# Convolution module of a two-layer encoder trunk: eleven more second-row taps on VectorE, and a written order for the totals, the diagonal products and the tiles at the module's end

## Chip, cores and metric

The kernel runs on one core of a Trainium2 chip. The metric is the device time in microseconds (us) of one execution, as the median of several runs.

## The reference

The program computes a trunk of two layers on 256 tokens of 1024 channels. Each layer is a feed-forward block, a mixer and a second feed-forward block, each behind an RMS norm. The mixer of the first layer is a convolution module, and the change lies in its second half:

```python
def conv_module(h, w_pw1, w_dw, g_norm, w_pw2):
    u = h @ w_pw1
    a, b = jnp.split(u, 2, axis=-1)
    u = a * jax.nn.sigmoid(b)
    u = lax.conv_general_dilated(u, w_dw[:, None, :], window_strides=(1,),
        padding=[(CONV_WIDTH - 1, 0)], feature_group_count=D_MODEL, ...)
    u = jax.nn.silu(rmsnorm(u, g_norm))
    return u @ w_pw2
```

The convolution is depthwise: each channel is the sum of 31 shifted copies of itself, each times a weight of its own. The norm needs, for each token, the sum of squares over all 1024 channels, so it can only be finished when the last channel of a token is.

## The kernel before

**Tiles.** In the module's middle the data lie with channels on partitions: eight groups k = 0 to 7 of 128 channels, and along the free axis 30 zeros and 256 tokens (tile `V`). The tokens are worked in two halves of 128, here the *first rows* (tb 0) and the *second rows* (tb 1). `Y` holds the convolution's result in the same layout.

**Who computes the taps.** A tap is one of the 31 shifted products. Three tables (lines 49 to 51 of the kernel before) give each engine its groups and taps.
- VectorE (DVE, `taps_dve`, L764 to L776): one multiply-add per tap (L775), into two accumulators `acc` in PSUM by turns, which L776 adds at the end. It has groups 0, 2, 4, 5 and taps 0 to 12 of group 7.
- ScalarE and GpSimd (ACT and POOL, `taps_pool`, L778 to L795): ACT writes each product into one of six buffers `prod` (L793), POOL adds it to `Y` or `part` and to `odd` by turns (L794), and L795 adds the two. They have groups 1, 3 and taps 0 to 18 of group 6.
- TensorE (PE, `taps_pe`, L797 to L807): a product with a diagonal matrix of the tap's weights, `diag`, summed in PSUM tile `y` (L804). It has the rest of groups 6 and 7: 12 + 18 products for each half of the tokens.

**The norm.** For a group and a half, L890 adds PE's part to the other engine's, ACT squares the result (L816, `sq`), and PE multiplies the squares with a column of ones (L822, tile `ms`): this is a *total*, and eight of them make the sum of squares of 128 tokens. Then `normed` (L835 to L854): DVE forms the mean (L838, `msc`), POOL raises it to the power -1/2 (L840, `rc`), DVE writes this on a diagonal (L842, `dg`), PE multiplies the diagonal with ones so that every partition has it (L844, `rb`), DVE multiplies each group with it (L849, `z`, six buffers), and ACT applies the Silu (L851, `Z`; for groups 0 to 3 also the rounded `Zh`, L853, whose remainder `Zl` DVE takes, L854). The groups come in the order 4 to 7, 0 to 3.

**The last product.** `mm` (L905) multiplies `Z` with the last weights, tile by tile in that order and two column halves each (L915, tile `o`); groups 0 to 3 take three passes (`lo` with `Zh`, `hi` with `Zh`, `hi` with `Zl`: L277, L280, L281). `add` (L921) adds the result to the residual `h`. The next feed-forward block then takes `h` in transposed pieces `tp` (L320, `Xh`, `Xl`), and its first two weight blocks must be split by ACT into `hi` (L164) and by DVE into `lo` (L168). `load_ahead()` calls for these.

**What sets the order.** Each engine works its own queue strictly as written in the program. A list scheduler writes these queues when the program is built, from the dependences and its own estimates. `@urgent` gives a function's instructions priority; `order(a, b)` puts a behind b on an engine, with no wait added; `behind(a)` puts a behind the last urgent instructions of its engine. Ahead of the change only few places are tied in this way: the last totals, `rb`, and two positions in the last product (L901 to L912).

Of the kernel before, what the change touches and what calls it, by code (L numbers as in the profile page):

```python
# [11 lines left out]
F32 = mybir.dt.float32  # L12
# [68 lines left out]
def trunk(ctx: ExitStack, tc: tile.TileContext, x, xt, pos, invf, gains, gfin, wdw,  # L81
# [633 lines left out]
    def conv_in(act, X, make_next):  # L715
# [37 lines left out]

        behind(nc.scalar.activation(small.tile([P, 1], F32, tag="silu", name="silu2"), neghalf, AF.Silu))
        load_to(conv_block[-4] + 1)
# [7 lines left out]

        def taps_dve(k, j0, j1, t):  # L764

            slot[0] ^= 1
            c = slice(slot[0] * S, slot[0] * S + t.stop - t.start)
            out = Y[:, k, t]
            for j in range(j0, j1):
                v, w = V[:, k, j + t.start:j + t.stop], dw[:, k, j:j + 1]  # L770
                y = acc[(j - j0) % 2][:, c]
                if j - j0 < 2:
                    nc.vector.tensor_scalar(y, v, w, None, op0=ALU.mult)
                else:
                    nc.vector.scalar_tensor_tensor(out if j == j1 - 1 else y, v, w, y, op0=ALU.mult, op1=ALU.add)  # L775
            nc.vector.tensor_add(out, acc[(j1 - j0) % 2][:, c], out)  # L776

        def taps_pool(k, j0, j1, t):  # L778

            if j1 - j0 < TAPS and k not in part:  # L780
                part[k] = act.tile([P, S], F32, name=uid("part"))
            if k not in odd:
                odd[k] = act.tile([P, S], F32, tag="odd", name=uid("odd"))
            y = [(part[k] if k in part else Y[:, k, :])[:, t], odd[k][:, t]]
            for j in range(j0, j1):
                v, w = V[:, k, j + t.start:j + t.stop], dw[:, k, j:j + 1]
                o = y[(j - j0) % 2]
                if j - j0 < 2:
                    nc.scalar.activation(o, v, AF.Copy, scale=w)
                else:  # L790
                    p = act.tile([P, S], F32, tag="prod", name=uid("prod"), bufs=6)
                    p = p[:, :t.stop - t.start]
                    nc.scalar.activation(p, v, AF.Copy, scale=w)  # L793
                    nc.gpsimd.tensor_tensor(o, o, p, op=ALU.add)  # L794
            nc.gpsimd.tensor_tensor(y[0], y[0], y[1], op=ALU.add)  # L795

        def taps_pe(t, done):  # L797

            b = bank("A", "y")
            y = {}  # L800
            for i, (k, j0, j1) in enumerate(CONV_PE):
                y[k] = b[:, i * P:(i + 1) * P]
                for j in range(j0, j1):
                    mm = nc.tensor.matmul(y[k], diag[k][:, j - j0, :], V[:, k, j + t.start:j + t.stop],  # L804
                                          start=(j == j0), stop=(j == j1 - 1))
                    done.append(mm)
            return y  # L807
# [5 lines left out]
        def square(k, t):  # L813
            if k not in sq:
                sq[k] = act.tile([P, S], F32, tag="sq", name=uid("sq"), bufs=4)
            nc.scalar.activation(sq[k][:, t], Y[:, k, t], AF.Square)  # L816

# [17 lines left out]
        def normed(tb, after=()):  # L835

            ms = small.tile([P, 1], F32, tag="msc", name=uid("msc"))
            nc.vector.tensor_scalar(ms, msb[tb][:, :1], 1.0 / D, EPS, op0=ALU.mult, op1=ALU.add)  # L838
            rc = small.tile([P, 1], F32, tag="rc", name=uid("rc"))
            nc.gpsimd.tensor_tensor(rc, ms, neghalf, op=ALU.pow)  # L840
            dg = act.tile([P, P], F32, tag="dg", name=uid("dg"), bufs=2)
            nc.vector.tensor_scalar(dg, ident, rc, None, op0=ALU.mult)  # L842
            rb = bank("AC"[tb], "rb")
# [3 lines left out]
            for k in rows_order:  # L847
                z = act.tile([P, P], F32, tag="z", name=uid("z"), bufs=6)
                nc.vector.tensor_mul(z, Y[:, k, tbs(tb)], rb[:, :P])  # L849
                g = G[:, g0 + k:g0 + k + 1]  # L850
                nc.scalar.activation(Z[:, k, tbs(tb)], z, AF.Silu, scale=g)  # L851
# [4 lines left out]
        for items, taps in ((CONV_DVE, taps_dve), (CONV_POOL, taps_pool)):  # L856
            for item in items:
                if item[0] in CONV_FIRST:
                    for tb in range(NT):
                        taps(*item, tbs(tb))  # L860
                elif item[0] not in CONV_LAST:
                    taps(*item, every)
        for k in CONV_ORDER:
# [4 lines left out]
        sums = {}  # L868
        for tb in range(NT):
            t = tbs(tb)  # L870
            for item in CONV_DVE:
                if item[0] in CONV_LAST:
                    taps_dve(*item, t)
            for item in CONV_POOL:
                if item[0] in CONV_LAST:
                    taps_pool(*item, t)
            if tb == 0:
                for k in CONV_ORDER:
                    if k not in CONV_LAST:
                        for i in range(NT):  # L880
                            total(k, i)
            y[tb] = taps_pe(t, done[tb])
        def ends(tb, after, after_row):
# [4 lines left out]
            def add():  # L888
                for k in CONV_LAST:
                    nc.vector.tensor_add(Y[:, k, t], y[tb][k], part[k][:, t] if k in part else Y[:, k, t])  # L890
                    square(k, t)
# [3 lines left out]

            add()
            normed(tb, (after_row,))


        n = len(done[1])  # L900
# [20 lines left out]
        def add(tb, d):  # L921
            c = slice(d * 512, d * 512 + 512)
            nc.vector.tensor_add(h[tb][:, c], o[tb, d], h[tb][:, c])

        nxt = None
        load_ahead()
# [260 lines left out]
    dw = const.tile([P, KT, TAPS], F32, name="dw")  # L1187
    diag = {}
    apart = ExitStack()
    dpool = apart.enter_context(tc.tile_pool(name="diag", bufs=1))  # L1190

    def diagonals():
        fetch(dw, wdw)
        for k, j0, j1 in CONV_PE:
            diag[k] = dpool.tile([P, j1 - j0, P], F32, name=f"diag{k}")
# [113 lines left out]
```

## Time and profile before

| what | us |
|---|---|
| median of 3 runs | 929.18 |
| the three runs | 929.18, 927.61, 929.3 |
| the profiled execution | 928.0 |
| its span, from the first to the last instruction | 926.2 |
| PE busy in the span | 913.4 |
| from the first totals to the next feed-forward block (243.79 to 288.43 of the span) | 44.64 |

The profile gives times from the span's start. In a timeline, a row is a run of alike instructions of one engine: its start, the time to the end of the last, line, operation, tiles, count, and in brackets how long the engine sat idle before it and what released it. A product in full float32 stands in the trace as two records, so x20 are ten products. Consecutive instructions overlap, so that the distance of two starts is less than the duration of one.

### The profile page before, as it was taken

What the parts mean: (1) busy time and instruction counts of PE and PEld (TensorE: products, weight loads), DVE (VectorE), ACT (ScalarE), POOL (GpSimd) and SP (SyncE); (2) the same over time, 40 slices, a digit from 0 to 9 for tenths busy, and PEclk for the clock granted to TensorE, in tenths of its full rate; (3) what the DMA queues carried; (4) which work ended last, traced back from release to release, by engine and by line L of the source; (5) the groups of instructions that cost most, each with busy time, mean ns of one, the idle gap of its engine ahead of it and who ended that gap; (6) DMA issues with size and microseconds to landing.
All of it is one profiled execution on the core that took longest, in us unless ns stands there. A gap on an engine that the chain in (4) does not pass through costs nothing.

```text
span 926.2 us, 12414 instructions
## 1 busy us (share of the span) xinstructions
PE 913.4 (99%) x4337; PEld 761.0 (82%) x4337; DVE 680.1 (73%) x1041; ACT 537.6 (58%) x930; POOL 222.0 (24%) x329
## 2 busy tenths in 40 slices
PE   8999999999999999999999999999999999999997
PEld 6888888898967888888888888888898778888886
DVE  5777787589975667777976667978666476667875
ACT  6965455568865554555574445655667374544643
POOL 0101232479920110232210003223200010003123
PEclk9999999999999999999999999999999999999999
DMA  9986656554324866566756765666451457774751
GB/s 338 346 280 228 222 162 227 227 183 142 133 91 154 298 230 229 183 196 210 296 218 237 231 242 174 204 215 240 182 183 46 182 206 239 252 247 144 230 181 46
DMA packets 60399, 191.58 MB, mean 207 GB/s; under 512 B 11184, under 2 KB 33328, under 8 KB 40752
## 3 DMA queue, kind: packets, MB, share of 16 engines
q1 hardware_dynamic: 59760, 190.09, 59.0%
q8 instruction: 34, 0.56, 0.2%
q10 hardware_dynamic: 576, 0.69, 0.2%
q14 instruction: 29, 0.24, 0.1%
HBM read 178.17 MB, written 12.58 MB: 206 GB/s over the span
## 4 chain that ended last, share of the span: by engine, by line
PE 89%; ACT 3%; DVE 3%; issue 1%; DMA 1%; POOL 1%; POOLq 0%; SPq 0%; ACTq 0%
PE u L281 17%; PE u L277 17%; PE u L280 17%; PE o L277 6%; PE o L280 6%; PE o L281 6%; PE gate L731 3%; PE u L731 3%; DVE lo L168 2%; PE p L277 2%; PE p L280 2%; PE p L281 2%; PE o L915 2%; ACT hi L164 1%; DMA raw<-in_f1w 1%
## 5 line engine op out<-in xcount | busy, mean ns | idle before, releaser
L168 DVE TENSOR_TENSOR lo<-raw,hi 128x1024 fp32r<-128x1024 f32 (+1 forms) x246 | 297.8, 1247 | 74.4 <-ACT hi L164 74.1
L164 ACT CAST hi<-raw 128x1024 fp32r<-128x1024 f32 (+1 forms) x250 | 248.0, 1046 | 151.7 <-PE u L281 112.3
L281 PE MATMUL u<-hi,Xl 128*128 128x512 f32 x688 | 267.8, 390 | 0.7 <-DVE Xl L338 0.7
L277 PE MATMUL u<-lo,Xh 128*128 128x512 f32 x688 | 268.1, 390 | 0.0
L280 PE MATMUL u<-hi,Xh 128*128 128x512 f32 x688 | 267.7, 389 | 0.0
L281 PEld LDWEIGHTS u<-hi,Xl 128*128 128x128 f32 x688 | 129.1, 188 | 28.3 <-DVE Xl L338 1.6
L277 PEld LDWEIGHTS u<-lo,Xh 128*128 128x128 f32 x688 | 129.1, 188 | 27.2 <-DVE lo L168 0.5
L280 PEld LDWEIGHTS u<-hi,Xh 128*128 128x128 f32 x688 | 129.1, 188 | 26.6
L178 POOL TENSOR_TENSOR sums<-raw 128x1024 f32<-128x1024 f32 x20 | 53.0, 2652 | 161.2 <-DMA raw<-in_f2w 54.7
L277 PE MATMUL o<-lo,Gh 128*128 128x512 f32 (+1 forms) x236 | 91.0, 386 | 0.0
L281 PE MATMUL o<-hi,Gl 128*128 128x512 f32 (+1 forms) x236 | 91.0, 386 | 0.0
L280 PE MATMUL o<-hi,Gh 128*128 128x512 f32 (+1 forms) x236 | 91.0, 385 | 0.0
L625 POOL TENSOR_TENSOR sx<-gb 128x128 f32<-128x128 f32 x20 | 10.2, 508 | 311.6 <-DMA gb<-gd 311.6
L617 ACT CAST Gh<-gb 128x512 fp32r<-128x512 f32 (+2 forms) x48 | 25.6, 540 | 54.6 <-DMA gb<-gd 54.6
L187 DVE TENSOR_TENSOR lo<-sums,hi 128x1024 fp32r<-128x1024 f32 x40 | 56.1, 1433 | 0.0
L618 DVE TENSOR_TENSOR Gl<-gb,Gh 128x512 fp32r<-128x512 f32 (+2 forms) x48 | 33.2, 705 | 28.8 <-ACT Gh L617 28.8
L775 DVE SCALAR_TENSOR_TENSOR acc<-V,dw,acc 128x256 f32<-128x256 f32 (+1 forms) x160 | 53.9, 418 | 0.0
L186 ACT CAST hi<-sums 128x1024 fp32r<-128x1024 f32 x40 | 40.7, 1051 | 22.6 <-PE u L281 15.0
L281 PEld LDWEIGHTS o<-hi,Gl 128*128 128x128 f32 x236 | 44.3, 188 | 9.0
L277 PEld LDWEIGHTS o<-lo,Gh 128*128 128x128 f32 x236 | 44.3, 188 | 8.9
L280 PEld LDWEIGHTS o<-hi,Gh 128*128 128x128 f32 x236 | 44.3, 188 | 8.8
L186 ACT CAST hi<-raw 128x512 fp32r<-128x512 f32 (+1 forms) x40 | 31.4, 834 | 32.9 <-PE o L281 26.6
(247 smaller groups left out, 1347.4 us busy)
## 6 DMA issues: line engine op xcount, KB each, us to landing
raw<-in_f2w SPq DMA_DIRECT2D x66, 1024.0 KB, 4.9
raw<-in_f1w SPq DMA_DIRECT2D x64, 1024.0 KB, 5.0
raw<-in_cw SPq DMA_DIRECT2D x12, 1024.0 KB, 5.1
gd<-gt SPq DMA_DIRECT2D x160, 64.0 KB, 2.6
gb<-gd SPq DMA_DIRECT2D x40, 256.0 KB, 2.9
raw<-in_wo SPq DMA_DIRECT2D x4, 1024.0 KB, 4.8
raw<-in_wuq SPq DMA_DIRECT2D x3, 1024.0 KB, 4.8
raw<-in_f1w SPq DMA_DIRECT2D x8, 256.0 KB, 6.7
```

What stands on the lines that cost most here:

```text
L164: behind(nc.scalar.copy(hi[:, c], raw[:, c]))
L168: behind(nc.vector.tensor_sub(lo[:, c], raw[:, c], hi[:, c].bitcast(F32)))
L178: behind(nc.gpsimd.tensor_tensor(t[:, 0:2, :], v[:, 0:4:3, :], v[:, 1:2, :].to_broadcast([P, 2, 512]), op=ALU.add))
L186: behind(nc.scalar.copy(hi[:, c0:c1], x[:, c0:c1]))
L187: behind(nc.vector.tensor_sub(lo[:, c0:c1], x[:, c0:c1], hi[:, c0:c1].bitcast(F32)))
L277: mm = nc.tensor.matmul(o, ah, bl, start=start, stop=False)
L280: nc.tensor.matmul(o, ah, bh, start=False, stop=False)
L281: return nc.tensor.matmul(o, al, bh, start=False, stop=stop)
L617: nc.scalar.copy(dh, x)
L618: nc.vector.tensor_sub(dl, x, dh.bitcast(F32))
L731: mm = nc.tensor.matmul(u[:, t], w[:, c], X.x[:, k, t], start=(k == 0), stop=(k == KT - 1))
L775: nc.vector.scalar_tensor_tensor(out if j == j1 - 1 else y, v, w, y, op0=ALU.mult, op1=ALU.add)
```

## The change

- **Taps.** The tables get a fourth column: the half of the tokens (0, 1, or 2 for both). In the second rows, group 7 gives taps 13 to 23 from PE to VectorE: PE has 12 + 7 products there in place of 12 + 18, VectorE 24 taps in place of 13.
- **Diagonal.** `dg` is written by ScalarE (Copy with a scale) and no longer by VectorE.
- **PE's order.** The diagonal products of the first rows come right behind the module's first half, with the totals of groups 3 and 5 at fixed places among them (`CONV_MID`); the second rows' products follow, and behind the fifth of them come the last totals of the first rows, behind the fourteenth `rb`.
- **VectorE's order.** The second-row taps of group 7 are tied one behind the other. The first comes behind the first rows' `Y`, the fifth behind the mean, the tenth behind the last `z` of the first rows.
- **ScalarE and GpSimd.** Products and their sums keep one order through all groups. From the second rows' tap 10 on, products come behind `dg` and sums behind the power. `odd` has a buffer each for even and odd groups. The load of the Silu table comes behind the seventh-tap product of group 6.
- **Second rows' norm.** It is called at the seventh of eight groups of the last product (before: at the third), so that the last totals, `rb` and the tiles of the second rows come later; `load_ahead()` and the first rows' `add` come behind them.

The core of the diff, without the lines that only pass a return value on:

```diff
-CONV_DVE = ((0, 0, 31), (2, 0, 31), (4, 0, 31), (5, 0, 31), (7, 0, 13))
-CONV_POOL = ((1, 0, 31), (3, 0, 31), (6, 0, 19))
-CONV_PE = ((6, 19, 31), (7, 13, 31))
+CONV_DVE = ((0, 0, 31, 0), (0, 0, 31, 1), (2, 0, 31, 2), (4, 0, 31, 2), (5, 0, 31, 2), (7, 0, 13, 0), (7, 0, 24, 1))
+CONV_POOL = ((1, 0, 31, 0), (1, 0, 31, 1), (3, 0, 31, 2), (6, 0, 19, 0), (6, 0, 19, 1))
+CONV_PE = ((6, 19, 31, 0), (7, 13, 31, 0), (6, 19, 31, 1), (7, 24, 31, 1))
+CONV_MID = {3: 10, 5: 29}
...
+                if j in after:
+                    order(ins, after[j].ins)
+                if j > j0 and after:
+                    order(ins, before.ins)
...
-                odd[k] = act.tile([P, S], F32, tag="odd", name=uid("odd"))
+                odd[k] = act.tile([P, S], F32, tag=f"odd{k % 2}", name=uid("odd"))
...
+                    if last_prod[0] is not None:
+                        order(prod, last_prod[0].ins)
+                        order(ins, last_sum[0].ins)
+                    if "power" in after and j >= j0 + 10:
+                        order(prod, after["diagonal"].ins)
+                        order(ins, after["power"].ins)
...
-            nc.vector.tensor_scalar(dg, ident, rc, None, op0=ALU.mult)
+            diagonal = nc.scalar.activation(dg, ident, AF.Copy, scale=rc)
...
+        taps(0)
+        order(silu, nc_silu[0].ins)
+        for k in CONV_ORDER:
+            if k not in CONV_LAST:
+                if k == [*CONV_MID][0]:
+                    y[0] = taps_pe(0, done[0])
+                    order(done[0][0], mm.ins)
+                for i in range(NT):
+                    mm = total(k, i)
+                    if k in CONV_MID:
+                        order(mm, done[0][CONV_MID[k]].ins)
...
-        ends(0, done[1][n // 2 + 1], done[1][n * 3 // 4 + 1])
+            steps_of.update({0: a, 4: mean, 9: z, "power": power, "diagonal": diagonal})
...
+        ends(0, done[1][4], done[1][13])
+        order(done[1][5], sums[0].ins)
+        order(done[1][14], brow[0].ins)
+        taps(1)
...
-                after = {4: [sums[1]], 6: [brow[1]]}[n] if n in (4, 6) else ()
+                after = [brow[1]] if n == KT - 1 else ()
...
-                if tb == 0 and f == 0:
+                if tb == 0 and f == 4:
                     first = now
-                if tb == 0 and f == 2:
-                    ends(1, first[1], now[1])
+                if tb == 0 and f == KT - 2:
+                    last_z = ends(1, first[1], now[1])
+                    load_ahead()
```

What this does to the queues is seen at three places. On PE, at the end of the first rows' norm, stood before (y_2542 are the second rows' products, ms_2429 the first rows' totals):

```order
L804 MATMUL y_2542<-V,diag_445 128x128 x10
L804 MATMUL y_2542<-V,diag_695 128x128 x5
L822 MATMUL ms_2429<-ones,sq_2574 128x1
L804 MATMUL y_2542<-V,diag_695 128x128 x3
L822 MATMUL ms_2429<-ones,sq_2577 128x1
L804 MATMUL y_2542<-V,diag_695 128x128 x10
L844 MATMUL rb_2587<-dg_2585,ones 128x128
L915 MATMUL o_2637<-raw_1908,Z 128x512
```

Now the same place on PE reads as follows (y_2474 are the second rows' products, and two more of them stand ahead of these rows in both programs):

```order
L826 MATMUL y_2474<-V,diag_445 128x128 x3
L844 MATMUL ms_2429<-ones,sq_2495 128x1
L844 MATMUL ms_2429<-ones,sq_2498 128x1
L826 MATMUL y_2474<-V,diag_445 128x128 x7
L826 MATMUL y_2474<-V,diag_695 128x128 x2
L866 MATMUL rb_2508<-dg_2506,ones 128x128
L826 MATMUL y_2474<-V,diag_695 128x128 x5
L954 MATMUL o_2621<-raw_1908,Z 128x512
```

The eleven products are gone, the two totals stand together behind five products, and `rb` has five products behind it where it had none.

On ACT, between the first rows' squares (sq) and the first Silu tiles (Z), stood before:

```order
L816 ACTIVATE sq_2577<-Y 128x128
L793 ACTIVATE prod_2532<-V,dw 128x128
L793 ACTIVATE prod_2535<-V,dw 128x128
L793 ACTIVATE prod_2538<-V,dw 128x128
L816 ACTIVATE sq_2574<-Y 128x128
L816 ACTIVATE sq_2577<-Y 128x128
L851 ACTIVATE Z<-z_2589,G 128x128
```

Here the last two squares are those of the second rows. Now ACT has, at the same place:

```order
L838 ACTIVATE sq_2498<-Y 128x128
L864 ACTIVATE dg_2506<-ident,rc_2504 128x128
L805 ACTIVATE prod_2593<-V,dw 128x128
L805 ACTIVATE prod_2596<-V,dw 128x128
L805 ACTIVATE prod_2599<-V,dw 128x128
L805 ACTIVATE prod_2602<-V,dw 128x128
L805 ACTIVATE prod_2605<-V,dw 128x128
L805 ACTIVATE prod_2608<-V,dw 128x128
L805 ACTIVATE prod_2611<-V,dw 128x128
L805 ACTIVATE prod_2614<-V,dw 128x128
L873 ACTIVATE Z<-z_2510,G 128x128
L873 ACTIVATE Z<-z_2513,G 128x128
```

Eight products of the second rows now stand between the diagonal and the first Silu tile; a ninth follows two tiles later.

On PE, at the end of the first rows' last product (o_2621 and o_2622; ms_2431 and rb_2661 belong to the second rows, o_2721 is their product), the change has:

```order
L280 MATMUL o_2622<-lo_1544,Zh 128x512
L844 MATMUL ms_2431<-ones,sq_2498 128x1
L283 MATMUL o_2622<-hi_1543,Zh 128x512
L284 MATMUL o_2622<-hi_1543,Zl 128x512
L280 MATMUL o_2622<-lo_1544,Zh 128x512
L283 MATMUL o_2622<-hi_1543,Zh 128x512
L284 MATMUL o_2622<-hi_1543,Zl 128x512
L866 MATMUL rb_2661<-dg_2659,ones 128x128
L280 MATMUL o_2621<-lo_1544,Zh 128x512
L283 MATMUL o_2621<-hi_1543,Zh 128x512
L284 MATMUL o_2621<-hi_1543,Zl 128x512
L954 MATMUL o_2721<-raw_1908,Z 128x512
```

Before, 15 such passes stood behind the second rows' `rb`, and 15 products (six in full float32, nine passes) between their last total and it; now there are three passes behind it and five between.

More of the change, by code (lines that the diff above doesn't have):

```diff
@@ L752, in conv_in @@
                 X.late((mm,))
-        behind(nc.scalar.activation(small.tile([P, 1], F32, tag="silu", name="silu2"), neghalf, AF.Silu))
+        silu = nc.scalar.activation(small.tile([P, 1], F32, tag="silu", name="silu2"), neghalf, AF.Silu)
+        nc_silu = []
         load_to(conv_block[-4] + 1)
@@ L854, in normed @@
                     nc.vector.tensor_sub(Zl[:, k, tbs(tb)], Z[:, k, tbs(tb)], Zh[:, k, tbs(tb)].bitcast(F32))
[L856 to L862, printed above, removed]
+            return mean, power, diagonal, zi
+        halves = (tbs(0), tbs(1), every)
+        for items, f in ((CONV_DVE, taps_dve), (CONV_POOL, taps_pool)):
+            for k, j0, j1, half in items:
+                if k not in CONV_LAST:
+                    f(k, j0, j1, halves[half])
         for k in CONV_ORDER:
@@ L1193, in diagonals @@
         fetch(dw, wdw)
-        for k, j0, j1 in CONV_PE:
+        for k, j0, j1, half in CONV_PE:
+            if half:
+                continue
+            first_tap[k] = j0
             diag[k] = dpool.tile([P, j1 - j0, P], F32, name=f"diag{k}")
```

78 lines of the change are left out of this document (44 added, 34 removed).

## Prediction

> **What bounds the kernel now.** I read the busy times first, then the chain that ended last, then PE's timeline at the place of the change.
>
> ```profile
> PE 913.4 (99%) x4337; PEld 761.0 (82%) x4337; DVE 680.1 (73%) x1041; ACT 537.6 (58%) x930; POOL 222.0 (24%) x329
> ...
> PE 89%; ACT 3%; DVE 3%; issue 1%; DMA 1%; POOL 1%; POOLq 0%; SPq 0%; ACTq 0%
> ```
>
> PE is busy for 99% of the span and makes 89% of the last chain. So a change pays here only if PE has less to do or waits less. Two stretches of the module's end (us, PE, PEld, DVE, ACT, POOL busy, then clock and DMA):
>
> ```profile
> 258.00:262.02 4.02, 2.97 (x25) 2.59 (x23) 3.18 (x14) 0.96 (x4) 2.58 (x7) 1.00 0.00 0
> 262.02:275.18 13.16, 13.15 (x47) 8.33 (x48) 9.52 (x25) 9.88 (x25) 0.55 (x1) 1.00 0.43 161
> ```
>
> PE is idle in the first of them, for 4.02 - 2.97 = 1.05 us. Its timeline shows where:
>
> ```profile
> 245.50 2.25 PE L804 MATMUL y<-V,diag 128*128 128x128 f32 x18
> ...
> 253.17 0.51 PE L822 MATMUL ms<-ones,sq 128*128 128x1 f32 x4
> 253.54 3.59 PE L804 MATMUL y<-V,diag 128*128 128x128 f32 x30
> 256.97 0.28 PE L822 MATMUL ms<-ones,sq 128*128 128x1 f32 x2
> ...
> 258.00 2.48 PE L804 MATMUL y<-V,diag 128*128 128x128 f32 x20
> 260.72 0.49 PE L844 MATMUL rb<-dg,ones 128*128 128x128 f32 x2 [0.24 <-DVE dg L842]
> 262.02 1.98 PE L915 MATMUL o<-raw,Z 128*128 128x512 f32 x4 [0.81 <-ACT Z L851]
> 263.85 0.50 PE L822 MATMUL ms<-ones,sq 128*128 128x1 f32 x4
> 264.21 5.40 PE L915 MATMUL o<-raw,Z 128*128 128x512 f32 x12
> 269.04 0.79 PE L277 MATMUL o<-lo,Zh 128*128 128x512 f32 x1
> 269.67 0.39 PE L280 MATMUL o<-hi,Zh 128*128 128x512 f32 x1
> 269.90 0.39 PE L277 MATMUL o<-lo,Zh 128*128 128x512 f32 x1
> ...
> 271.50 0.38 PE L844 MATMUL rb<-dg,ones 128*128 128x128 f32 x2
> ...
> 275.18 7.03 PE L915 MATMUL o<-raw,Z 128*128 128x512 f32 x16
> ```
>
> The second rows' diagonal products run out at 258.00 + 2.48 = 260.48. Then PE waits 0.24 for `dg`, does `rb` alone, and waits 0.81 for the first `Z`. The second rows' `rb` at 271.50 costs no wait, since PE has work behind it until 275.18.
>
> **What the change takes away.** Fifteen diagonal products take 256.97 - 253.54 = 3.43 us, or 0.229 each; eleven fewer are -2.52 us on the engine that sets the end. The two idle times, -1.05, go if other work stands there. And `rb` no longer stands alone: its 0.49, and the 0.19 by which the last product's end at 260.48 lies behind its share (258.00 + 10 x 0.229 = 260.29), become about 0.18 in a stream, as for one of the two totals that hold it up by 0.37 (253.17 to 253.54). That is -0.5. Together -4.07 us, if nothing new is waited for. That has to be tested in three places.
>
> **First rows: when are the totals ready?** VectorE's rows:
>
> ```profile
> 250.49 2.67 DVE L775 SCALAR_TENSOR_TENSOR acc<-V,dw,acc 128x128 f32<-128x128 f32 x10
> 253.07 0.34 DVE L775 SCALAR_TENSOR_TENSOR Y<-V,dw,acc 128x128 f32<-128x128 f32 x1
> 255.15 0.29 DVE L890 TENSOR_TENSOR Y<-y,part 128x128 f32<-128x128 f32 x1 [1.74 <-POOL part L795]
> ...
> 259.10 0.15 DVE L838 TENSOR_SCALAR msc<-ms 128x1 f32<-128x1 f32 x1
> ...
> 260.20 0.47 DVE L842 TENSOR_SCALAR dg<-ident,rc 128x128 f32<-128x128 f32 x1 [0.69 <-POOL rc L840]
> ...
> 261.25 1.67 DVE L849 TENSOR_TENSOR z<-Y,rb 128x128 f32<-128x128 f32 x8
> ...
> 264.38 0.16 DVE L838 TENSOR_SCALAR msc<-ms 128x1 f32<-128x1 f32 x1
> ...
> 265.20 0.29 DVE L842 TENSOR_SCALAR dg<-ident,rc 128x128 f32<-128x128 f32 x1 [0.25 <-POOL rc L840]
> ```
>
> Before, VectorE sat 1.74 us until POOL had group 6 of the first rows. POOL's rows:
>
> ```profile
> 242.87 0.46 POOL L794 TENSOR_TENSOR part<-part,prod 128x128 f32<-128x128 f32 x1 [1.76 <-ACT prod L793]
> ...
> 247.09 0.99 POOL L794 TENSOR_TENSOR odd<-odd,prod 128x128 f32<-128x128 f32 x2 [0.47 <-ACT odd L789]
> ...
> 254.66 0.46 POOL L795 TENSOR_TENSOR part<-part,odd 128x128 f32<-128x128 f32 x1
> 255.07 0.46 POOL L794 TENSOR_TENSOR part<-part,prod 128x128 f32<-128x128 f32 x1
> ...
> 259.61 0.55 POOL L840 TENSOR_TENSOR rc<-msc,neghalf 128x1 f32<-128x1 f32 x1
> ```
>
> POOL lost 1.76 + 0.47 waiting for ACT (the Silu table's load and the shared `odd`), and its queue held six sums of the second rows ahead of its end at 254.66 + 0.46 = 255.12, at 0.41 each (255.07 - 254.66). The fixed order removes both: 255.12 - 2.23 - 2.48 = 250.4. The next to be late is then PE: 30 first-row products from 245.50 with two totals among them (0.37, from 253.17 to 253.54) are issued by 252.7 and end 0.16 later. The sum that reads them (now L922) therefore starts at about 252.9, where VectorE arrives at 252.55, after eight of the ten taps; three taps at 0.258 (253.07 - 250.49, over ten), the sum of the accumulators and group 7's sum bring the last square to about 254.95. PE reaches its last total at 254.35, so it waits **+0.6** there.
>
> **First rows: the new wait for Z.** On VectorE four taps (1.03) stand ahead of the mean, which starts at about 255.6. From there the chain of before counts: mean to power to `dg` took 0.15 + 0.08 + 0.55 + 0.03, so `dg` starts at 256.4. PE is then still in its products and does not wait for `rb`. But on ACT eight products follow `dg` before the first `Z`. What one costs:
>
> ```profile
> 242.34 0.97 ACT L793 ACTIVATE prod<-V,dw 128x128 f32<-128x128 f32 x3
> ```
>
> ```profile
> L793 ACT ACTIVATE prod<-V,dw 128x128 f32<-128x128 f32 x82 | 29.8, 396 | 1.5 <-POOL odd L794 0.6 <-POOL Y L794 0.3
> L1197 ACT ACTIVATE diag<-ident,dw 128x128 f32<-128x128 f32 x30 | 9.3, 390 | 0.0
> ```
>
> The mean duration is 0.396, but three in a row take 0.97, so the distance is (0.97 - 0.39) / 2 = 0.29. I take 0.29, because no POOL wait stands there: six buffers are free and POOL resumes with the power. `dg` and eight products are 9 x 0.29 = 2.6, so the first `Z` starts at 259.0, ends 0.39 later, and the last product starts at **259.45**, against 262.02: -2.57. PE is free at about 258.45, so it waits **+1.0**. (The sum of the terms: -4.07 + 0.6 + 1.0 = -2.47; the 0.1 between them is rounding.) Were each product 0.396, as the end for the range, this wait were 0.85 longer; were ACT no limit, `Z` would start 0.3 after `z`, itself 261.25 - 260.72 = 0.53 behind `rb`, and the wait fell by about 0.8.
>
> [...]
>
> **The diagonal on ACT.** On VectorE `dg` would now stand behind second-row taps at 0.258 each; on ACT it costs like the diagonals of L1197, 0.39. On VectorE the two `dg` took 0.47 and 0.29, so the move is between -0.1 and +0.1 in each chain; I take nothing. [...]
>
> **Second rows.** VectorE does 24 taps, eight `z`, four `Zl` and three sums from 254.6 on. With `z` at 0.2 (1.67 for eight), two `z` held back until ACT frees one of six buffers, and the rest at 0.2 to 0.26, it ends at about 265.5. PE reaches the last total much later. Eight tile products in full float32 take 269.04 - 262.02 less 0.36 for the two totals among them (263.85 to 264.21), 6.66; the first pass 0.63, each further one 0.23 (269.90 - 269.67); with 16 passes and one total ahead of it that is 6.66 + 0.63 + 3.45 + 0.18 = 10.9 behind 259.45, at 270.35. So 4.8 us are to spare and the eleven added taps (2.8 us) are hidden. POOL, which now stands still from its eighth second-row sum until the power, ends at about 261, half a microsecond ahead of VectorE's need. But five passes and the total itself hide only 1.3 us until `rb`, and the chain took 264.38 - 264.03 = 0.35 to the mean (264.03 is the second total of the row at 263.85), 0.16 + 0.08 + 0.55 + 0.03 to `dg`, 0.39 + 0.05 to `rb`: 1.6. **+0.25**. And from `rb` to the first use of `Z` passed 262.02 - 260.72 = 1.3 us, where `rb` and three passes (0.27 from `rb` to a steady pass, an estimate from the 0.38 of its row at 271.50, and 0.69) are about 0.95: **+0.35**. So +0.6.
>
> **Behind it.** The casts of the next block's weights move behind the second rows' tiles:
>
> ```profile
> 265.10 3.87 ACT L164 CAST hi<-raw 128x1024 fp32r<-128x1024 f32 x4
> ...
> 283.71 2.17 ACT L334 ACTIVATE Xh<-tp,G 128x128 fp32r<-128x128 f32 x8 [6.62 <-PE tp L320]
> ```
>
> ```profile
> 268.54 2.60 SPq L161 DMA_DIRECT2D raw<-in_f2w  x2
> ...
> 278.80 3.76 SPq L161 DMA_DIRECT2D raw<-in_f2w  x2
> ```
>
> ACT sat 6.62 us ahead of `Xh`. With `Z` from 272.6 to 276.1, casts (3.87) and two squares (1.3) it is free at 281.3, and the pieces `tp` end at 281.9: covered by 0.6 us. If that cover goes, `Xh` and the feed-forward block follow one for one, with 0.4 us between `Xl` and the block's first use. The block's third to sixth weight blocks, asked for at 268.5 to 282.6 before, come at about 276 to 282; their casts wait for PE to free earlier weights at 286 and later, so I cost this at nothing.
>
> **Sum.** -4.07 + 0.6 + 1.0 + 0.6 = -1.87, or -1.97 by the starts themselves: **-1.9 us**, and everything behind moves with PE. The profiled execution, 928.0 (span 926.2 and 1.8 around it), becomes 926.1. The four executions shown (929.18, 927.61, 929.3 and 928.0) have a mean of 928.5, so a median of new runs lies 0 to 1.2 above the profiled one; I add 0.4 and predict **926.5**.
>
> **Rivals.**
> - *The chain clears* (0.22): `Z` follows its `z` at once and the second rows wait half as long, so 0.8 + 0.3 less is lost: -3.0, and 925.4 with the same 0.4. For it speaks that before nothing stood between `z` and `Z`, which PE got 262.02 - 261.25 = 0.77 behind the first `z`; against it the eight products in the queue.
> - *The gain is mostly waited away* (0.23): products cost 0.396 in the queue (+0.85): -1.05, 927.4. For it speaks that 0.396 is the mean duration of 82; against it the 0.97 for three.
> - *Slower* (0.07): POOL. Its sums now keep ACT's order without passing one another. If they starve, group 6 of the first rows is late; beyond 252.9, 2.5 us behind my 250.4, each microsecond moves the mean, `dg`, the eight products and `Z`, and it becomes slower from 2.5 + 1.9 = 4.4 us on. At a delay of 6 us: +1.6, 930.0. Against it: the longest wait of POOL for ACT here was 1.76, and its cause has moved.
> - *The change does not do what it says* has no room: PE's queue holds eleven products fewer.
>
> **How the numbers follow.** My forecast has 0.48, at 925.9 to 927.1. 0.2%, 1.86 us, is about what a measurement of this kernel can tell from no change. The forecast lies just beyond it, so I give 0.30 of its 0.48 to faster; with the first rival 0.52 faster, 0.18 + 0.23 = 0.41 within, 0.07 slower. The range goes from the first rival with the rest of its waits gone by half (925.4 - 0.9) to the second with the largest offset of the runs (927.4 + 0.8): 924.5 to 928.2.
>
> **What would show it.** In the profile after: 49 in place of 60 diagonal products; POOL's first-row end near 250.4; a PE wait near 0.6 at the last first-row total and near 1.0 for the first `Z`; the last product from 259.45 and its second half from 273.2; short waits at the second `rb` and `Z`; the feed-forward block from about 286.5. Wrong if `Z` starts right behind `z`, if POOL waits for ACT again, or if PE idles at the block's start.

## The result, and the profile after

The changed kernel takes 927.33 us (median of 12 runs, 926.02 to 927.98), the kernel before on the same chip 929.14 (927.32 to 929.91): a ratio of 0.998, 95% interval 0.9971 to 0.9989, or **1.81 us less**. The profiled execution of the changed kernel is the longest of its twelve, 927.98 with a span of 926.2. Its span therefore equals that of before, and the gain must be read from the stage. PE's rows of the changed kernel there (start, us, line, tiles, count, and in brackets the idle time ahead):

```profile
PE 912.5 (99%) x4315; PEld 757.9 (82%) x4315; DVE 682.2 (74%) x1050; ACT 537.2 (58%) x932; POOL 224.9 (24%) x329
```

```profile
245.52 1.84 PE L844 MATMUL ms<-ones,sq 128*128 128x1 f32 x16
...
256.02 0.28 PE L844 MATMUL ms<-ones,sq 128*128 128x1 f32 x2
256.89 0.38 PE L844 MATMUL ms<-ones,sq 128*128 128x1 f32 x2 [0.59 <-ACT sq L838]
257.14 2.25 PE L826 MATMUL y<-V,diag 128*128 128x128 f32 x18
...
259.23 0.39 PE L866 MATMUL rb<-dg,ones 128*128 128x128 f32 x2
259.45 1.28 PE L826 MATMUL y<-V,diag 128*128 128x128 f32 x10
...
261.27 7.13 PE L954 MATMUL o<-raw,Z 128*128 128x512 f32 x16 [0.54 <-ACT Z L873]
...
272.15 0.28 PE L844 MATMUL ms<-ones,sq 128*128 128x1 f32 x2
...
273.73 0.49 PE L866 MATMUL rb<-dg,ones 128*128 128x128 f32 x2
...
275.04 7.13 PE L954 MATMUL o<-raw,Z 128*128 128x512 f32 x16
...
288.40 0.39 PE L280 MATMUL u<-lo,Xh 128*128 128x512 f32 x1
```

And of the kernel before, the stage's two ends and the last first-row totals:

```profile
243.79 1.84 PE L822 MATMUL ms<-ones,sq 128*128 128x1 f32 x16
...
256.97 0.28 PE L822 MATMUL ms<-ones,sq 128*128 128x1 f32 x2
257.11 0.91 PE L804 MATMUL y<-V,diag 128*128 128x128 f32 x6
...
288.43 0.40 PE L277 MATMUL u<-lo,Xh 128*128 128x512 f32 x1
```

PE has 22 records fewer (4337 - 4315), the eleven products. The first totals stand 1.73 us later than in the execution of before (245.52 against 243.79), the feed-forward block at the same place: the stage fell from 44.64 to 42.88 us, **1.76 less**, as the medians say. Counted from the first totals, the last product starts at 15.75 (before 18.23), its second half at 29.52 (31.39). The 0.24 ahead of the first rows' `rb` is gone, and the wait for the first `Z` is 0.54 where it was 0.81. Two short waits are new: 0.59 ahead of the last first-row total, and the stretch from the second rows' last total to their `Z`, where PE runs out of passes.

I take the first totals' start for no effect of an edit; with one profiled execution of each kernel this is not shown. In the 14 executions profiled in this study it lies anywhere from 242.44 to 245.62, while from the block to the end it is always 637.7 to 638.2 us. The times of one kernel spread as far: the kernel before took 926.57 to 929.97 on one chip. Part of the spread is seen: between 140 and 180 us PE stood idle for 0.70 us in the changed kernel, in two waits for `lo`, VectorE's half of a weight block, and not at all in the kernel before. So distances within the stage tell kernels apart more finely than times do. Each distance is from one execution; the 15.75 of the change returns in e3, e4 and e6.

### The profile page after: what moved, and what is told of

It reads as the page before. It is cut to its first block, busy times and chain, and to the rows that moved or that the text cites. A ratio compares the mean times of both kernels' runs of the same rounds, so it can differ in the third digit from the quotient of the medians.

```text
span 926.2 us, 12404 instructions
## 1 busy us (share of the span) xinstructions
PE 912.5 (99%) x4315; PEld 757.9 (82%) x4315; DVE 682.2 (74%) x1050; ACT 537.2 (58%) x932; POOL 224.9 (24%) x329
## 4 chain that ended last, share of the span: by engine, by line
PE 85%; DVE 5%; ACT 3%; DMA 3%; issue 2%; POOL 1%; SPq 0%; POOLq 0%; ACTq 0%; DVEq 0%
PE u L284 16%; PE u L280 16%; PE u L283 16%; PE o L280 5%; PE o L283 5%; PE o L284 5%; DVE lo L171 3%; PE gate L734 3%; PE u L734 3%; DMA raw<-in_f1w 2%; PE o L954 2%; PE p L280 1%; PE p L283 1%; PE p L284 1%; ACT hi L167 1%
## 5 line engine op out<-in xcount | busy, mean ns | idle before, releaser
L779 DVE SCALAR_TENSOR_TENSOR acc<-V,dw,acc 128x128 f32<-128x128 f32 (+1 forms) x171 | 57.5, 416 | 0.0
```

The source lines that it names most:

```text
L779: ins = nc.vector.scalar_tensor_tensor(out if j == j1 - 1 else y, v, w, y, op0=ALU.mult, op1=ALU.add)
```

## Experiments

All numbers in one table: the first totals' start in the span, then distances from there (us), and the median beside that of the kernel before on the same chip.

| kernel | first totals | last product | second half | block | median | before | ratio, 95% |
|---|---|---|---|---|---|---|---|
| before | 243.79 | 18.23 | 31.39 | 44.64 | | | |
| changed | 245.52 | 15.75 | 29.52 | 42.88 | 927.33 | 929.14 | 0.9980 (0.9971-0.9989) |
| e1 taps back | 244.90 | 17.51 | 30.86 | 44.22 | 927.31 | 927.67 | 0.9996 (0.9986-1.0005) |
| e9 taps alone | 243.71 | 18.52 | 35.08 | 48.34 | 930.85 | 927.67 | 1.0030 (1.0020-1.0039) |
| e13 e9, idle filled | 244.45 | 26.28 | 39.34 | 52.60 | 935.65 | 927.18 | 1.0086 (1.0071-1.0102) |
| e8 three taps back | 244.09 | 15.75 | 29.20 | 42.55 | 925.62 | 927.84 | 0.9976 (0.9967-0.9984) |
| e2 held from tap 14 | 243.73 | 15.04 | 28.72 | 42.08 | 925.22 | 927.67 | 0.9972 (0.9963-0.9981) |
| e3 held from tap 6 | 242.71 | 15.75 | 29.74 | 43.10 | 925.97 | 927.18 | 0.9987 (0.9978-0.9996) |
| e5 diagonal on VectorE | 243.53 | 15.04 | 28.82 | 42.17 | 925.10 | 927.84 | 0.9974 (0.9966-0.9983) |
| e4 second norm earlier | 243.55 | 15.75 | 28.92 | 42.18 | 925.17 | 927.67 | 0.9967 (0.9955-0.9980) |
| e6 POOL's edits undone | 242.93 | 15.75 | 29.51 | 42.87 | 925.64 | 927.18 | 0.9980 (0.9971-0.9989) |
| e10 sums last | 242.44 | 15.17 | 28.93 | 42.29 | 924.61 | 927.84 | 0.9967 (0.9955-0.9979) |
| e7 e2 and e4 | 243.52 | 15.04 | 28.10 | 41.36 | 924.33 | 927.84 | 0.9964 (0.9952-0.9976) |
| e11 e2, e4 and e10 | 245.62 | 14.67 | 27.83 | 41.09 | 924.92 | 927.18 | 0.9971 (0.9961-0.9980) |

My theory was: PE's eleven products are the gain, the order makes room for it, and three short waits of PE (for the last first-row total, the first `Z` and the second rows) take part of it back. The rival: the order makes the gain by itself.

### e1: the order without the taps

```diff
-CONV_DVE = (..., (7, 0, 24, 1))
-CONV_PE = (..., (7, 24, 31, 1))
+CONV_DVE = (..., (7, 0, 13, 1))
+CONV_PE = (..., (7, 13, 31, 1))
```

> Order kept, the eleven taps given back from VectorE to PE. On PE they stand behind the first rows' rb. My theory (the gain is PE's eleven products, and the order only makes room for it): +2.52 of products, less the 0.54 of waiting for Z that they cover, is +2.0: the last product starts 17.7 us behind the first totals (15.75 in the changed kernel, 18.23 before), the feed-forward block 44.9 (42.88 and 44.64), time about 929.3. Rival (the order made the gain, the taps little): block at 43.4 or earlier, time 927.8 or less.

The block comes at 44.22: 1.34 behind the changed kernel, 0.42 ahead of the kernel before. The eleven products cost (262.41 - 258.83) / 16 = 0.224 each, 2.46 in all:

```profile
258.61 0.39 PE L866 MATMUL rb<-dg,ones 128*128 128x128 f32 x2
258.83 3.74 PE L826 MATMUL y<-V,diag 128*128 128x128 f32 x32
262.41 7.03 PE L954 MATMUL o<-raw,Z 128*128 128x512 f32 x16
```

They fill the wait for `Z` (0.71 by e2, below), and the second rows' last total comes earlier, with fourteen passes between it and `rb` in place of five, which gives back 0.42 of their wait (13.35 between the halves, 13.77 in the change): 2.46 - 0.71 - 0.42 = 1.33. So the order alone is worth 0.4 of the stage, where the rival had 1.2 or more; the times by themselves don't tell e1 from the kernel before. My expectation of 44.9 missed by 0.7: it counted 0.54 for the wait for `Z` and left the second rows out.

### e9: the taps without the order

```diff
+SECOND = {13: 24}
-                for j in range(j0, j1):
+                j0 = SECOND.get(a, a) if t.start else a
+                for j in range(j0, j1):
...
-                    taps_dve(*item, t)
+                    taps_dve(*item[:2], SECOND.get(item[2], item[2]) if tb else item[2], t)
```

> The kernel before with the eleven taps moved to VectorE and nothing else: no new order, diagonal on VectorE, second rows' norm at the third group. My theory (PE's products in this place were cover for the first rows' norm, so without a new order a wait takes their place): PE stands idle for some 3 us ahead of rb, four taps stand ahead of the diagonal and three more and a sum ahead of the first z on VectorE; the last product starts 18.2 to 19.0 us behind the first totals (18.23 before), and the second rows, whose last total and rb now come later, cost up to 1.5 more: block at 44.6 to 46.5, time 929 to 931. Rival (eleven products fewer are 2.5 us wherever they go): block at 42.1, time 926.6.

The same eleven products fewer, and it is **slower**: 3.70 us in the stage. (The places of the first rows' totals and `rb` are set as shares of the number of second-row products, and move with it; all 19 products are done ahead of the last total.) PE's rows, then the stretches (us, PE, PEld, DVE, ACT, POOL busy, granted clock, DMA):

```profile
257.55 0.28 PE L824 MATMUL ms<-ones,sq 128*128 128x1 f32 x2
260.63 0.49 PE L846 MATMUL rb<-dg,ones 128*128 128x128 f32 x2 [2.79 <-DVE dg L844]
262.23 3.78 PE L917 MATMUL o<-raw,Z 128*128 128x512 f32 x4 [1.11 <-ACT Z L853]
...
277.07 0.49 PE L846 MATMUL rb<-dg,ones 128*128 128x128 f32 x2 [0.18 <-DVE dg L844]
```

```profile
260.60:261.20 0.60, 0.49 (x2) 0.30 (x2) 0.60 (x3) 0.00 (x0) 0.00 (x0) 1.00 0.00 0
261.20:261.40 0.20, 0.00 (x0) 0.00 (x0) 0.20 (x2) 0.08 (x1) 0.00 (x0) 0.93 0.00 0
261.40:262.20 0.80, 0.00 (x0) 0.00 (x0) 0.80 (x5) 0.66 (x3) 0.00 (x0) 0.50 0.00 0
...
268.00:268.20 0.20, 0.20 (x2) 0.20 (x1) 0.20 (x1) 0.20 (x2) 0.00 (x0) 0.50 0.00 0
268.20:268.40 0.20, 0.20 (x1) 0.06 (x1) 0.20 (x1) 0.20 (x2) 0.00 (x0) 1.00 0.00 0
```

Up to the last product the expectation holds: 2.52 of products are gone, and 2.79 - 0.24 and 1.11 - 0.81 of waiting take their place (2.85 together), so it starts 0.29 later. The second loss I did not expect. PE's four records of the last product take 3.78 us where they took 1.98 before: the granted clock stands at 0.50 from 261.37 (0.93 is 0.17 of 0.2 us at full clock) to 268.2. PE works in it from 262.23 on, 5.97 us at half speed, of which half, 2.98, are lost by this estimate. That is most of the 3.40 by which the second half is later (16.56 behind the start, 13.16 before); the other 0.4 lies between the second rows' last total, done at 275.40, and their `rb`: VectorE's mean now stands behind the residual's sum and starts at 275.92. All ten executions of e9 have a mean granted clock of 0.994 to 0.996 and those of the kernel before 0.997 to 0.999, so the fall is not that of one execution.

### e13: does filled idle time keep the clock?

```diff
+        fill = bank("C", "fill")
+        for j in range(18):
+            last_fill = nc.tensor.matmul(fill[:, :P], diag[CONV_LAST[1]][:, j, :], V[:, CONV_LAST[1], j:j + P], start=True, stop=True)
+            order(last_fill, (sums if j < 11 else brow)[0].ins)
+            if j < 11:
+                order(brow[0], last_fill.ins)
```

The 18 products go to a PSUM tile that nobody reads.

> The kernel before with the taps moved and nothing else (which lost 3.2 us), and in addition 18 products whose result nobody reads, on PE where it stood idle: 11 ahead of rb and 7 behind it. VectorE does four more taps and two sums ahead of the first z, and the second rows' totals and rb stand again where they did before. My theory (there the granted clock fell to 0.50 for 6 us because PE had stood idle for 2.8 us, and that cost about 3): the clock stays at 1.00, the last product starts 19.8 to 20.3 behind the first totals (18.52 without the products), its second half 13.2 to 13.5 behind that (16.56), block at 46.2 to 47.2 (48.34), so that useless work makes it faster. Rival (the clock fell for another reason, or the loss was the late rb of the second rows): the clock falls again, second half 15.5 or more behind, block at 48.5 or later.

This failed as a test: the products waited themselves, since their PSUM tile came free only when VectorE had added its accumulators.

```profile
263.73 5.06 PE L906 MATMUL fill<-V,diag 128*128 128x128 f32 x22 [5.16 <-DVE Y L777]
```

```profile
262.40:262.60 0.20, 0.00 (x0) 0.00 (x0) 0.20 (x2) 0.00 (x1) 0.00 (x0) 0.76 0.00 0
...
269.20:269.40 0.20, 0.20 (x4) 0.20 (x3) 0.14 (x1) 0.00 (x0) 0.00 (x0) 0.67 0.00 0
```

PE stood idle for 5.16 us instead of 2.79, and the clock fell again, to 0.50 from 262.50 to 269.33. So it is a second case of a fall behind idle time. That filled time would have kept the clock, and with it that idle time alone is the cause, wasn't shown.

### e8: three of the eleven taps back on PE

```diff
-(7, 0, 24, 1) ... (7, 24, 31, 1)
+(7, 0, 21, 1) ... (7, 21, 31, 1)
```

> The changed kernel with three of the eleven taps given back to PE, behind rb. My theory (PE waits there anyway for Z): 3 x 0.229 = 0.69 of products fill the wait of 0.54 (0.68 between starts), so the last product starts 15.75 to 15.9 behind the first totals; the second rows' total comes no earlier: block at 42.9, no change. So eight moved taps are worth as much as eleven in this order. Rival (each product given back costs its 0.229): start 16.4, block 43.6, time 0.7 more.

The last product starts at 15.75 as in the change: three products for nothing, since PE waits for `Z` there in the change. The block is even 0.33 earlier, which I had not expected. With VectorE's taps fewer, the scheduler put the second rows' last total two passes further ahead, so that seven passes cover the chain to `rb` instead of five (rows of e8; compare 272.15 and 273.73 above):

```profile
270.25 0.28 PE L844 MATMUL ms<-ones,sq 128*128 128x1 f32 x2
...
272.09 0.38 PE L866 MATMUL rb<-dg,ones 128*128 128x128 f32 x2
```

### e2, e3 and e5: what makes the first Z late

```diff
-                    if "power" in after and j >= j0 + 10:
+                    if "power" in after and j >= j0 + 14:
```

> The changed kernel with ACT's products held back behind the diagonal only from tap 14 on (tap 10 in the change): four products fewer between the diagonal and the first Z. My theory (the queue of eight products makes PE wait for Z): the first Z starts right behind its z, PE's wait of 0.54 goes, the last product starts 15.2 us behind the first totals (15.75), the block 42.3 (42.88), time 926.8. Rival (the chain of mean, power, diagonal and rb sets the first Z, or POOL's four further sums hold the power up): start at 15.7 or later, no gain.

The wait is gone, and the last product starts 0.71 earlier (15.04). In the changed kernel ACT had eight products ahead of the first `Z`; here it has five, three fewer and not four as expected, and `Z` starts 0.32 behind its `z` (257.86), in the change 1.18 (259.65). ACT's rows of the change, then of e2:

```profile
258.19 0.40 ACT L864 ACTIVATE dg<-ident,rc 128x128 f32<-128x128 f32 x1 [1.35 <-POOL rc L862]
258.50 2.43 ACT L805 ACTIVATE prod<-V,dw 128x128 f32<-128x128 f32 x8
260.83 0.68 ACT L873 ACTIVATE Z<-z,G 128x128 f32<-128x128 f32 x2
```

```profile
256.39 0.40 ACT L864 ACTIVATE dg<-ident,rc 128x128 f32<-128x128 f32 x1 [1.35 <-POOL rc L862]
256.70 1.55 ACT L805 ACTIVATE prod<-V,dw 128x128 f32<-128x128 f32 x5
258.18 1.57 ACT L873 ACTIVATE Z<-z,G 128x128 f32<-128x128 f32 x5
```

e5 takes the same wait away in another manner:

```diff
-            diagonal = nc.scalar.activation(dg, ident, AF.Copy, scale=rc)
+            diagonal = nc.vector.tensor_scalar(dg, ident, rc, None, op0=ALU.mult)
```

> The changed kernel with the diagonal back on VectorE, in both halves. There it stands behind four second-row taps and comes about 0.3 later, as rb does (PE has cover for that only in part: rb may be late by up to 0.3); but ACT no longer waits for the power and does the eight products from 257 on, so that Z follows its z at once. My theory (eight products behind the diagonal cost the wait, the diagonal's own engine nothing): last product starts 15.2 to 15.5 behind the first totals (15.75), second half 13.6 to 13.8 behind (13.77), block 42.2 to 42.6. Rival (the move to ACT was the gain): rb later by 0.3 or more on PE's path, start at 15.9 or later, block 43.0 or later.

It starts at 15.04 too. The diagonal on VectorE takes 0.28, and ACT, which need not wait for the power, does the eight products ahead of `z`, so that `Z` starts 0.33 behind it (257.65):

```profile
256.48 0.28 DVE L864 TENSOR_SCALAR dg<-ident,rc 128x128 f32<-128x128 f32 x1
```

```profile
254.75 2.75 ACT L805 ACTIVATE prod<-V,dw 128x128 f32<-128x128 f32 x8
257.98 0.40 ACT L873 ACTIVATE Z<-z,G 128x128 f32<-128x128 f32 x1 [0.48 <-DVE z L871]
```

The wait was ACT's queue, not the time that the diagonal takes on either engine. So one edit of the change cost 0.71 as it was queued: with `dg` on ACT, the products tied behind it wait for the power (ACT is idle for 1.35 ahead of `dg`, in the change as in e2). I expected `rb` 0.3 later; it came at 13.70 as before (13.71), since PE's nine products end only then. The diagonal itself is shorter on VectorE (0.28, on ACT 0.40), but e2 has the same start with it on ACT.

e3 was to be the dose the other way:

```diff
-                    if "power" in after and j >= j0 + 10:
+                    if "power" in after and j >= j0 + 6:
```

> The changed kernel with products held back from tap 6 on (tap 10 in the change): four more products between the diagonal and the first Z. My theory (each costs its distance of 0.29, all of it in PE's wait for Z): +1.17, the wait 1.7, the last product starts 16.9 behind the first totals (15.75), block at 44.0. Rivals: at 0.396 each +1.6, start at 17.35; or Z is set by its z and nothing changes, 15.75.

It tells nothing on ACT's products. The scheduler left the same eight ahead of the first `Z` and put the others between and behind the tiles; the start stayed at 15.75. That is the number of the second rival, but not for its reason: `Z` still stands behind the eight products and not right behind its `z`. The block came 0.22 later, with a wait of 0.27 ahead of the second rows' `rb`, since their totals moved towards it: four passes stand between the last of them and `rb`, five in the change.

### e4: the second rows' norm earlier

```diff
-            if (tb, d) == (0, 0):
-                after = [brow[1]] if n == KT - 1 else ()
+            if tb == 0:
+                after = [sums[1]] if n in (5, 6) else [brow[1]] if n == KT - 1 else ()
...
-                if tb == 0 and f == 4:
+                if tb == 0 and f == 2:
...
-                if tb == 0 and f == KT - 2:
+                if tb == 0 and f == KT - 4:
```

> The changed kernel with the second rows' norm earlier in the first rows' last product: totals behind the fifth group, rb behind the seventh, so that twelve passes stand between total and rb (five in the change) and six behind rb (three). My theory (the second rows' wait is missing cover, since VectorE is done with them 4 us earlier): from the last product's start to its second half 13.2 us (13.77 in the change, 13.16 before), block at 42.3, time 926.8. Rival (VectorE with 24 taps isn't done by then, and PE waits at the total): 13.8 or longer, no gain.

From the start to the second half it is now 13.17 us, in place of 13.77 (13.16 before): the whole wait of 0.6 is gone. PE's rows, and VectorE's last sum of the second rows, 2.3 us ahead of the totals:

```profile
267.65 0.50 PE L844 MATMUL ms<-ones,sq 128*128 128x1 f32 x4
...
270.86 0.38 PE L866 MATMUL rb<-dg,ones 128*128 128x128 f32 x2
...
272.47 7.03 PE L954 MATMUL o<-raw,Z 128*128 128x512 f32 x16
```

```profile
265.09 0.29 DVE L922 TENSOR_TENSOR Y<-y,Y 128x128 f32<-128x128 f32 x1
```

### e6: POOL's two edits undone

```diff
-                odd[k] = act.tile([P, S], F32, tag=f"odd{k % 2}", name=uid("odd"))
+                odd[k] = act.tile([P, S], F32, tag="odd", name=uid("odd"))
...
-        order(silu, nc_silu[0].ins)
+        behind(silu)
```

> The changed kernel with two of its edits undone: `odd` has one buffer again, and the Silu table's load stands where it stood before. My theory (these edits end POOL's waits of 2.2 us, but POOL is done with group 6 of the first rows 2.3 us ahead of the sum that reads it, 252.46 against 254.72): no loss or up to 0.3, block at 42.9 to 43.2. Rival (they carry part of the gain): the first-row sum is late by 1 us or more, start of the last product at 16.5 or later, block at 43.7 or later.

No loss: 42.87. POOL's last first-row sum starts 6.92 behind the first totals (249.85 - 242.93), 0.44 later than in the change (252.00 - 245.52 = 6.48), and VectorE asks for it only at 9.20. Before it started at 10.87 (254.66 - 243.79), so 3.95 of POOL's gain of 4.39 come without these two edits. The written order of products and sums is the likely cause; no run undoes it alone. Rows of e6, then of the change:

```profile
249.85 0.46 POOL L816 TENSOR_TENSOR part<-part,odd 128x128 f32<-128x128 f32 x1
```

```profile
252.00 0.46 POOL L816 TENSOR_TENSOR part<-part,odd 128x128 f32<-128x128 f32 x1
```

### e10: group 6's sum behind VectorE's last taps

```diff
                     a = nc.vector.tensor_add(Y[:, k, t], y[tb][k], part[k][:, t] if k in part else Y[:, k, t])
+                    if tb == 0:
+                        order(a, last_tap[0].ins)
```

> The changed kernel with group 6's sum of the first rows on VectorE placed behind the three last taps of group 7 and the sum of its accumulators (in the change ahead of them, where VectorE sits 0.35 idle for PE's y). My theory (the 0.59 at the last first-row total is VectorE's end): the last square comes 0.35 earlier, PE waits 0.25 there; PE's products behind are the same, and the wait for Z stays (the mean stands behind four taps, and all of it moves by 0.35): last product starts 15.4 behind the first totals (15.75), block 42.5. Rival (the wait is ACT's two squares, which now stand close together): no gain, 42.9.

PE's idle time ahead of the last first-row total is gone, the 0.54 for `Z` stays, and the last product starts 0.58 earlier, more than the 0.35 of idle time. VectorE's rows of the change, then of e10 (252.50 - 242.44 = 10.06 behind the first totals, 10.63 in the change):

```profile
254.72 0.29 DVE L922 TENSOR_TENSOR Y<-y,part 128x128 f32<-128x128 f32 x1 [0.35 <-PE y L826]
...
255.82 0.29 DVE L785 TENSOR_TENSOR Y<-acc,Y 128x128 f32<-128x128 f32 x1
256.15 0.29 DVE L922 TENSOR_TENSOR Y<-y,Y 128x128 f32<-128x128 f32 x1
```

```profile
252.09 0.29 DVE L785 TENSOR_TENSOR Y<-acc,Y 128x128 f32<-128x128 f32 x1
252.30 0.28 DVE L923 TENSOR_TENSOR Y<-y,part 128x128 f32<-128x128 f32 x1
252.50 0.28 DVE L923 TENSOR_TENSOR Y<-y,Y 128x128 f32<-128x128 f32 x1
```

Beside the 0.35 (0.44 between starts, since eight taps at 0.258 from 252.22 on would let the sum start at 254.28), two dependent sums no longer stand back to back: 0.33 from L785 to the sum that needs it, 0.21 where another stands between.

### e7 and e11: the gains together

e7 has the edits of e2 and e4, e11 that of e10 as well.

> The two gains together: products held back from tap 14 on, and the second rows' norm earlier (totals behind the fifth group, rb behind the seventh). My theory (two separate waits of PE): the last product starts 15.0 us behind the first totals as with the first alone, and its second half 13.2 behind that as with the second alone: block at 41.4 (42.08 and 42.18 alone, 42.88 in the changed kernel), 1.5 us less than the changed kernel. Rival (an earlier first half makes PE wait for VectorE's second rows instead): second half 13.6 or more behind, block at 41.9 or later.

> Three edits on the changed kernel together: products held back from tap 14 on, second rows' norm earlier, and group 6's first-row sum behind VectorE's last taps. My theory (three separate waits of PE, each gone with its edit): no wait of PE is left between the first totals and the feed-forward block; the last product starts 14.45 behind the first totals (15.04 without the third edit), its second half 13.1 behind that, the block at 40.8 (41.36 with two edits, 42.88 in the changed kernel, 44.64 before), time 923.7 by the 0.6 less than the two. Rival (with the total earlier, Z is late behind the four products left, or the sixth group's end): start at 14.8 or later, block at 41.1 or later.

e7 comes at 41.36, as expected (41.4): the two waits are separate. e11 comes at 41.09, 0.27 better where 0.6 was expected: the block at the rival's figure (41.1), the start, at 14.67, between mine (14.45) and the rival's (14.8). POOL's four added sums now hold the power up, and so `dg`, the five products and the first `Z`: the mean is there at 256.91 + 0.15, the power starts 0.44 later, right behind the last sum, where in e2 and in e4, whose edits e7 joins, it started 0.08 behind the mean, and 0.07 in e10, which has the total as early and four sums fewer. What this costs the start was not tested alone (POOL, ACT and PE of e11):

```profile
257.09 0.45 POOL L807 TENSOR_TENSOR odd<-odd,prod 128x128 f32<-128x128 f32 x1
257.50 0.55 POOL L863 TENSOR_TENSOR rc<-msc,neghalf 128x1 f32<-128x1 f32 x1
```

```profile
258.39 1.55 ACT L806 ACTIVATE prod<-V,dw 128x128 f32<-128x128 f32 x5
259.85 1.56 ACT L874 ACTIVATE Z<-z,G 128x128 f32<-128x128 f32 x5
```

```profile
260.29 1.98 PE L957 MATMUL o<-raw,Z 128*128 128x512 f32 x4
```

Both beat the kernel before by 0.3 to 0.4% and the changed kernel by 1.5 and 1.8 us of the stage; their times can't be told from each other.

## Why the prediction held, point by point

- **Eleven products fewer, -2.52.** The products cost 0.224 each in e1, 2.46 in all. Of that the moved taps keep 1.34 with the order (44.22 - 42.88); alone they lose 3.7 us (e9), some 3.0 of it by the clock, and the order alone gains 0.4 (e1). The products removed were also the cover of the first rows' norm, and the gain of 1.76 belongs to neither part alone.
- **POOL's first-row end at 250.4.** In the change it ended at 252.46, 250.73 without the 1.73 by which this execution is late. So the end was hit, but not its split, and that is luck: the step put 2.23 of the gain to the Silu load and `odd` and 2.48 to the sums ahead; e6 shows 0.44 for the former.
- **Last first-row total, +0.6.** The idle time is 0.59, and its cause is VectorE's order (e10). But PE lost more than its idle time: the two last totals take 257.14 - 256.02 = 1.12 between starts, where one took 0.14 before (256.97 to 257.11), so 0.84 are lost.
- **First Z, +1.0 with eight products at 0.29.** The distance is right: (2.43 - 0.39) / 7 = 0.29, and so is the path of `Z`: without the 1.73, `dg` comes at 256.46 and the first `Z` at 259.10, predicted 256.4 and 259.0. The wait is mis-sized: 0.54 idle, 0.71 between the starts of e2 and the change. PE was free later than reckoned: e2, which doesn't wait, starts at 15.04, where -4.07 + 0.6 make 18.23 - 3.47 = 14.76. Of these 0.28, 0.24 are what the last total cost beyond its 0.6, and 0.04 are `rb`, which takes 0.22 between starts (259.23 to 259.45) for the 0.18 reckoned. The start itself was hit, 261.27 - 1.73 = 259.54 for 259.45, because `Z` sets it and not PE's own work.
- **The diagonal on ACT, nothing.** It takes 0.40 there, as reckoned. What it costs is in the wait for `Z`: e5 undoes the move and has 0.71 less.
- **Second rows, +0.6.** 13.77 - 13.16 = 0.61, and e4 takes all of it away. It is missing cover, as reckoned. The second half comes at 273.31 without the 1.73, predicted 273.2.
- **What lies behind, nothing.** ACT had 0.69 to spare ahead of `Xh`, predicted 0.6. Only a tenth was lost, since the second half's first products follow the tiles as they come (7.13 in place of 7.03).
- **Sum, -1.9 on the profiled execution.** The stage has -1.76.
- **From the profiled execution to the median, +0.4.** This term was off the most: the runs of before have a median of 929.14, 1.14 above the profiled 928.0. With it, 928.0 - 1.76 + 1.14 = 927.4, as measured (927.33); the predicted 926.5 is 0.8 below. So the measured time lies outside 925.9 to 927.1, where the forecast itself stood, and inside the range around it.
- **Rivals.** "The chain clears" is what e2 and e4 make of the kernel, not the change. The second rival's 927.4 is nearer to the measured time than my 926.5, but only by that last term: its -1.05 in the stage stands against -1.76, and products at 0.396 each are refuted by the 2.43 for eight. POOL had 2.3 us to spare, and e6 loses nothing.

## What to carry to other kernels

The work taken off the busiest engine had been the cover of a dependent chain: it lost 3.70 us in the stage without a new order (e9) and gained 1.76 with one. So look at what stood between the chain's links before you move it, and write the order of both together. Then look at each short wait that remains: here three edits of one to five lines, on queue positions alone, doubled the gain in the stage (3.55 for 1.76). Compare distances within the stage, where a time has a spread of 3 us.

## What the runs showed of the hardware

The granted clock fell to 0.50 in the middle of a kernel that had run at 1.00 (from 255 to 261.2 us in e9, to 262.4 in e13), after PE had stood idle for 2.79 us (e9) and 3.93 us (e13). In e9 PE's last product ended at 257.83; 3.54 us later, with 0.49 us of `rb` in between, the clock was halved for 6.83 us, though PE was busy from 262.23 on. In e13 the last one ended at 258.57, the clock fell 3.93 later, and again for 6.83 us. The kernel before, idle for 0.24 and 0.81 at this place, kept 1.00. Both 6.83 are estimates from the slices of 0.2 us in which the clock changes (0.93 in e9; 0.76 and 0.67 in e13). What sets this length, and how long PE must be idle before the clock falls, was not shown: between the 0.81 of the kernel before and the 2.79 of e9 nothing was tried.
